# Two weight splits put behind the even tokens' normed x in a two-layer hybrid encoder

## The chip, the cores and the metric

The kernel runs on one core of one Trainium2 chip. The metric is the device time of one execution in microseconds (us), taken as the median of several runs. The profile is one further execution of the same program, recorded by the hardware profiler; its times count from the start of its span. PE is the matrix engine (TensorE), PEld its weight loads, DVE the vector engine, ACT the scalar engine, POOL the GpSimd engine and SP the engine whose queue issues most DMAs.

## The reference

A trunk of two layers on x of 1 x 256 x 1024 in float32. Each layer has two sub-layers, and each begins with an RMSNorm. The core of it:

```python
def _rmsnorm(x, g):
    xf = x.astype(jnp.float32)
    y = xf * lax.rsqrt(jnp.mean(xf * xf, axis=-1, keepdims=True) + EPS)
    return (y * g.astype(jnp.float32)).astype(x.dtype)

def _token_mixer(xn, w_in, w_pool, pool_scale, w_a, w_b, w_o, rel_bias):
    u, q, k, v, g_pool, g_attn = jnp.split(xn @ w_in, SPLITS, axis=-1)
    ...
    merged = jax.nn.sigmoid(g_pool) * (pool_out @ w_a) + jax.nn.sigmoid(g_attn) * (attn_out @ w_b)
    return merged @ w_o

def _conv_ffn(xn, w_up, conv_w, conv_b, w_down):
    a, gval = jnp.split(xn @ w_up, 2, axis=-1)
    ...
    return (jax.nn.gelu(a) * gval) @ w_down

def reference(x, ...):
    h = x
    for layer in range(DEPTH):
        h = h + _token_mixer(_rmsnorm(h, norm1[layer]), ...)
        h = h + _conv_ffn(_rmsnorm(h, norm2[layer]), ...)
    return _rmsnorm(h, norm_f)
```

The weights are some 170 MB in float32, and each is read once.

## The kernel before

**Products in parts.** A float32 operand is cut into a high part, rounded to the matrix engine's fast float32 form (fp32r), and a low part, the rest. A product is the sum of three: high by high, high by low and low by high. The activations stand as `x2`, 8 chunks of 128 channels, each with its two parts and with the 128 even and the 128 odd tokens apart (`t` = 0 and 1).

**Weights.** The class `Weights` brings them in a fixed order. `load` issues a DMA of 1 MB into one of three `raw` buffers (L137, on SP's queue), and each raw is split in two pieces: ACT copies the piece to `wh` (L201) and DVE subtracts that from the raw to get `wl` (L203, 128x1024). Five pairs of wh and wl buffers exist; some first pieces of a stage go into idle tiles instead, whose names are those of their tags (`m2`, `v1`, `ybig`, `at2`), so that the profile calls them m, v, ybig and at. `get` takes the next piece and splits up to three ahead. A raw buffer is free for the next load when both its pieces are split, so the load after next waits for the last DVE subtraction from it.

**Order within an engine.** Each engine runs its instructions in the order of its own program. That order is decided when the kernel is built, by a scheduler which takes the instructions by the times it reckons with. `tc.issue_after(inst)` adds a constraint to it: an instruction made in that block and on `inst`'s engine comes behind `inst` in that engine's program. It adds no wait on a semaphore. `queue_behind(insts, n)` notes such ties for the next `n` pieces that are split: every instruction in `insts` ties the part of the split that lies on its own engine. At most four such notes are kept.

**The residual product and the norm behind it.** `residual_mm` multiplies by `w_o` (8 chunks) or `w_down` (22 chunks) into four PSUM tiles, for two token parities and two halves of the 1024 columns. The last four chunks are held back and done parity by parity, in segments of columns: 512 and 512 for the even tokens, 512, 256 and 256 for the odd ones (PE L585 to L587). Behind each segment `Norm.add` runs: DVE adds the sum to h (L445), ACT squares it with a sum (L447, and its read-out as a second instruction), and POOL adds to the mean square (L454, L456). After the last segment of a parity POOL raises it to the power -1/2 (L459, tile `rstd`). For the third segment DVE first folds the sum of the early chunks into h (L631).

**The normed x.** The generator `fin` in `to_channels` follows. DVE multiplies h by rstd and the gain in four quarters of 256 columns (L472, `xn`), PE transposes four chunks of 128 columns into PSUM (L481, `xt_ps`), ACT copies them to the high part of x2 (L484) and DVE takes the low part (L485); then the same for the other four chunks. The generator stops once between the two halves, and `residual_mm` puts work between: for the even tokens, the odd tokens' last segment; for the odd tokens, the last step of `fill`. `fill` (`begin_mlp` or `begin_values`) starts the next stage for the even tokens: `v_sum` (L667) multiplies their x2 by four held pieces, 6 products a piece, in the order high x by wh, high x by wl, low x by wh. After the odd tokens come the same four pieces for them.

**Where it stands.** This norm with its transposes runs three times: in layer 0 behind w_o, at about 238 to 256 us of the span (called the first place below), in layer 0 behind w_down, at about 421 to 440 us (the second), and in layer 1 behind w_o, at about 663 to 680 us (the third). The final norm has a code of its own. Before the change `fin` ties the six pieces after it to the odd tokens' last copy and subtraction, and nothing to the even tokens'.

Of the kernel before, what the change touches and what calls it, by code (L numbers as in the profile page):

```python
# [241 lines left out]
def encoder(ctx, tc, x, w_in, w_pool, pool_scale, w_a, w_b, w_o, norm1, norm2, w_up, conv_w,  # L242
# [11 lines left out]
    W = Weights(tc, wpool, big)  # L254
# [208 lines left out]
    def to_channels(x2, psum, g):  # L463

        tag = "acc" if psum is acc else "mm"

        def fin(t, r, xn):
            for n in range(4):  # L470
                cc = slice(n * 256, (n + 1) * 256)
                nc.vector.scalar_tensor_tensor(  # L472
                    out=xn[:, cc], in0=h[:, t, cc], scalar=r[:, 0:1], in1=g[:, cc],
                    op0=ALU.mult, op1=ALU.mult,
                )
            for n in range(2):
                pt = psum.tile([P, 4, P], F32, tag=tag, name="xt_ps")
                ks = slice(4 * n, 4 * n + 4)
                for k in range(4):
                    c0 = (4 * n + k) * P  # L480
                    nc.tensor.transpose(pt[:, k, :], xn[:, c0 : c0 + P], ident)  # L481
                oh, ol = (x2[:, ks, part, t, :] for part in (0, 1))
                last = [
                    nc.scalar.copy(out=oh, in_=pt),  # L484
                    nc.vector.tensor_sub(out=ol, in0=pt, in1=oh.bitcast(F32)),  # L485
                ]
                if n == 0:
                    yield
            if t == 1:
                W.queue_behind(last, 6)  # L490

        return fin

# [870 lines left out]
```

## Time and profile before

| | |
|---|---|
| median of 3 runs | 862.62 us (862.19 to 862.68) |
| profiled execution | 862.26 us, with a span of 860.5 us |
| PE busy | 852.6 us (99%) |
| DVE busy | 618.8 us (72%) |
| ACT busy | 492.8 us (57%) |
| POOL busy | 32.7 us (4%) |
| HBM traffic | 216 GB/s over the span |
| granted PE clock | 0.999 of full speed |

Matmuls overlap in the records: one of 128x512 shows some 0.39 us, while the next begins 0.23 us after it. So a stretch of PE work is read from the starts of its instructions, and a "busy" PE can still wait. On DVE and ACT too an instruction may begin some 0.1 us before the recorded end of the one before.

### The profile page before, as it was taken

The numbers are of one execution on the slowest core, as the hardware profiler recorded it, in microseconds if no ns is written. First come the engines' busy times: TensorE is split into PE (matmuls) and PEld (weight loads), VectorE is DVE, ScalarE is ACT, GpSimd is POOL, SyncE is SP. The second block draws the span as 40 slices with busy tenths as digits, with TensorE's granted clock in tenths as the row PEclk, the third lists the DMA queues.
The fourth block names the chain that finished last, engine by engine and source line by source line (L and its number), as shares of the span: only waits on it lengthen the run. The fifth ranks groups of instructions, "written<-read, shape, count | busy, mean of one in ns | idle before, by whom it ended". The sixth has DMA issues, their size and how long they took to land.

```text
span 860.5 us, 11694 instructions
## 1 busy us (share of the span) xinstructions
PE 852.6 (99%) x4343; PEld 728.3 (85%) x4343; DVE 618.8 (72%) x946; ACT 492.8 (57%) x770; POOL 32.7 (4%) x98
## 2 busy tenths in 40 slices
PE   9999999999999999999999999999999999999997
PEld 8888888888888888888888889888888888888886
DVE  7998786557766787777755987764666766876774
ACT  7656665555445566566545666664554555755662
POOL 1800000000010000000000000000000100000001
PEclk9999999999999999999999999999999999999999
DMA  9686556776747786566626565657876387775741
GB/s 335 210 254 200 196 177 227 240 265 197 256 157 247 269 276 236 196 237 203 244 98 200 187 202 195 207 182 250 274 238 246 131 274 237 267 256 182 243 147 49
DMA packets 136384, 186.80 MB, mean 217 GB/s; under 512 B 5560, under 2 KB 88192, under 8 KB 136328
## 3 DMA queue, kind: packets, MB, share of 16 engines
q1 hardware_dynamic: 136168, 185.79, 64.4%
q8 instruction: 34, 0.56, 0.3%
q10 hardware_dynamic: 160, 0.27, 0.1%
q14 instruction: 22, 0.18, 0.1%
HBM read 172.39 MB, written 13.65 MB: 216 GB/s over the span
## 4 chain that ended last, share of the span: by engine, by line
PE 95%; DVE 2%; ACT 1%; issue 1%; DMA 1%; POOL 0%; POOLq 0%; ACTq 0%
PE proj_ps L543 33%; PE t_ps L667 30%; PE v_ps L667 6%; PE res_ps L587 5%; PE res_ps L585 5%; PE res_ps L586 5%; PE v_ps L895 3%; PE v_ps L802 1%; PE pool_ps L543 1%; PE o_ps L1083 1%; PE s_ps L1034 1%; PE s_ps L1029 1%; PE o_ps L1079 1%; DVE h L445 1%; DMA raw<-in_w_in_dram 1%
## 5 line engine op out<-in xcount | busy, mean ns | idle before, releaser
L203 DVE TENSOR_TENSOR wl<-raw,wh 128x1024 fp32r<-128x1024 f32 x274 | 331.9, 1220 | 134.8 <-ACT wh L201 109.0
L201 ACT CAST wh<-raw 128x1024 fp32r<-128x1024 f32 x274 | 284.9, 1050 | 132.4 <-PE t_ps L667 64.7
L543 PE MATMUL proj_ps<-x,wh 128*128 128x512 f32 x832 | 196.9, 390 | 0.0
L543 PEld LDWEIGHTS proj_ps<-x,wh 128*128 128x128 f32 x832 | 154.3, 188 | 30.9
L667 PE MATMUL t_ps<-wh,x 128*128 128x512 f32 x576 | 180.1, 390 | 0.0
L667 PEld LDWEIGHTS t_ps<-wh,x 128*128 128x128 f32 x576 | 108.2, 188 | 22.4
L667 PE MATMUL t_ps<-wl,x 128*128 128x512 f32 x288 | 112.0, 389 | 0.0
L543 PEld LDWEIGHTS proj_ps<-x,wl 128*128 128x128 f32 x832 | 105.4, 191 | 3.0
L543 PE MATMUL proj_ps<-x,wl 128*128 128x256 f32 x832 | 107.8, 283 | 0.0
L586 PE MATMUL res_ps<-wl,actq 128*128 128x512 f32 (+1 forms) x184 | 69.9, 380 | 0.0
L587 PE MATMUL res_ps<-wh,actk 128*128 128x512 f32 (+1 forms) x184 | 69.9, 380 | 0.0
L585 PE MATMUL res_ps<-wh,actq 128*128 128x512 f32 (+1 forms) x184 | 69.7, 381 | 0.0
L667 PEld LDWEIGHTS t_ps<-wl,x 128*128 128x128 f32 x288 | 54.1, 188 | 11.1
L667 PE MATMUL t_ps<-wh,po 128*128 128x512 f32 x128 | 41.4, 395 | 0.0
L587 PEld LDWEIGHTS res_ps<-wh,actk 128*128 128x128 f32 x184 | 34.6, 188 | 6.6
L586 PEld LDWEIGHTS res_ps<-wl,actq 128*128 128x128 f32 x184 | 34.6, 188 | 6.4
L585 PEld LDWEIGHTS res_ps<-wh,actq 128*128 128x128 f32 x184 | 34.5, 188 | 6.3
L579 ACT COPY a<-proj_ps 128x256 f32<-128x256 f32 x36 | 13.8, 388 | 37.4 <-PE proj_ps L543 37.4
L580 DVE TENSOR_TENSOR a<-proj_ps,a 128x256 f32<-128x256 f32 x36 | 15.0, 423 | 24.5 <-ACT a L579 24.4
L454 POOL TENSOR_SCALAR ss<-ss 128x1 f32<-128x1 f32 x8 | 1.9, 236 | 781.8 <-ACT junk L447 781.8
L667 PEld LDWEIGHTS t_ps<-wh,po 128*128 128x128 f32 x128 | 24.0, 188 | 4.9
L447 ACT ACTIVATE junk<-h 128x512 f32<-128x512 f32 (+1 forms) x19 | 10.5, 554 | 29.6 <-DVE h L445 29.5
(204 smaller groups left out, 1101.0 us busy)
## 6 DMA issues: line engine op xcount, KB each, us to landing
raw<-in_w_in_dram SPq DMA_DIRECT2D x58, 1024.0 KB, 5.8
raw<-in_w_up_dram SPq DMA_DIRECT2D x44, 1024.0 KB, 6.1
raw<-in_w_down_dram SPq DMA_DIRECT2D x22, 1024.0 KB, 4.9
raw<-in_w_a_dram SPq DMA_DIRECT2D x8, 1024.0 KB
raw<-in_w_o_dram SPq DMA_DIRECT2D x8, 1024.0 KB, 7.1
crossing<-crossing SPq DMA_DIRECT2D x12, 512.0 KB, 5.1
turning<-turning SPq DMA_DIRECT2D x8, 512.0 KB, 2.7
turned_p<-turning SPq DMA_DIRECT2D x32, 128.0 KB, 3.3
```

The costliest lines, as they stand in the source:

```text
L201: inst = nc.scalar.copy(out=h, in_=src)
L203: inst = nc.vector.tensor_sub(out=l, in0=src, in1=h.bitcast(F32))
L445: nc.vector.tensor_add(out=h[:, t, cc], in0=ps, in1=h[:, t, cc])
L447: nc.scalar.activation(junk[:, 0 : cc.stop - cc.start], h[:, t, cc], AF.Square, scale=D**-0.5, accum_out=ss[:, n : n + 1],)
L543: nc.tensor.matmul(out, w(k), x, start=(steps is first and k == 0), stop=(steps is last and k == nk - 1), skip_group_check=turns["rest"],)
L579: nc.scalar.copy(out=out, in_=sums[1])
L580: nc.vector.tensor_add(out=out, in0=sums[0], in1=out)
L585: nc.tensor.matmul(ps, ah, wh, start=first, stop=False, skip_group_check=on)
L586: nc.tensor.matmul(ps, ah, wl, start=False, stop=False, skip_group_check=on)
L587: nc.tensor.matmul(ps, al, wh, start=False, stop=last, skip_group_check=on)
L667: nc.tensor.matmul(ps, x2[:, 2 * n + j, part, t, :], w[:, j, :], start=(n + m == 0), stop=(n == last and m == 5),)
L895: nc.tensor.matmul(ps[t], a[:, k, t, :], w[:, j, :], start=(k + m == 0), stop=(k == KD - 1 and m == 2),)
```

## The change

`fin` now calls `queue_behind` after each parity, not after the odd tokens alone.

```diff
@@ -486,8 +486,7 @@
                 ]
                 if n == 0:
                     yield
-            if t == 1:
-                W.queue_behind(last, 6)
+            W.queue_behind(last if t else last[1:], 6 if t else 2)
 
         return fin
```

For the even tokens (`t` = 0) the next two pieces to be split are tied, and to `last[1:]` alone, the DVE subtraction of the low part of the second half (L485). So the DVE part of these two splits (L203) must come behind it in DVE's program; ACT's copies (L201) are not tied. For the odd tokens the tie is as before. In the built programs, PE, ACT, POOL and SP have the same instructions in the same order before and after. DVE's order differs at the three places, where one weight subtraction moves at each; the second of the two tied pieces already stood behind. In the first and the third place:

```
before                          after
L631 h (odd, second quarter)    L631 h
L203 wl                         L485 x (even, first half)
L485 x (even, first half)       L445 h (odd, last segment)
L445 h (odd, last segment)      L485 x (even, second half)
L485 x (even, second half)      L203 wl
L472 xn (odd) x4                L472 xn x4
```

In the second place:

```
before                          after
L445 h (even, first segment)    L445 h (even, first segment)
L203 wl                         L445 h (even, second segment)
L445 h (even, second segment)   L472 xn (even) x3
L472 xn (even)                  L445 h (odd, first segment)
L445 h (odd, first segment)     L472 xn (even)
L472 xn (even) x3               ...
...                             L485 x (even, second half)
L485 x (even, second half)      L203 wl
L472 xn (odd) x4                L472 xn (odd) x4
```

The waits on semaphores stay the same but for those that follow from the new order. On SP's queue, in the first and the third place, the load that takes the raw buffer from which this `wl` is made waits for it as before, and so for an instruction that stands later.

## The prediction
> **What bounds the kernel.** I read the page first: its span, its chain of waits, then the waits of PE.
>
> ```profile
> span 860.5 us, 11694 instructions
> PE 95%; DVE 2%; ACT 1%; issue 1%; DMA 1%; POOL 0%; POOLq 0%; ACTq 0%
> raw<-in_w_up_dram SPq DMA_DIRECT2D x44, 1024.0 KB, 6.1
> ```
> ```profile
> PE v_ps L667 <- DVE x L485: 0.8, 2, 0.4
> PE xt_ps L481 <- DVE xn L472: 0.5, 1, 0.5
> ```
>
> PE carries 95% of the chain, so only what PE waits for can be won. The second fence (engine, what it waited for, us, times, longest) has the two waits on DVE, at the three norms the change touches: twice a product waits for the low part of x, once a transpose for xn. A gap in the records is smaller than the loss, because a record outlasts the start of the next one. I therefore take losses from starts, in the timeline of PE at the first place:
>
> ```profile
> 245.10 0.60 PE L481 MATMUL xt_ps<-ident,xn 128*128 128x128 f32 x4
> 245.45 0.36 PE L585 MATMUL res_ps<-wh,m 128*128 128x256 f32 x1
> ...
> 247.33 0.71 PE L667 MATMUL v_ps<-v,x 128*128 128x512 f32 x2
> 248.43 1.20 PE L667 MATMUL v_ps<-v,x 128*128 128x512 f32 x4 [0.39 <-DVE x L485]
> 249.46 1.53 PE L667 MATMUL v_ps<-ybig,x 128*128 128x512 f32 x6
> ...
> 252.19 0.60 PE L481 MATMUL xt_ps<-ident,xn 128*128 128x128 f32 x4
> ...
> 252.86 0.40 PE L667 MATMUL v_ps<-wl,x 128*128 128x512 f32 x1
> ...
> 254.37 1.64 PE L667 MATMUL v_ps<-v,x 128*128 128x512 f32 x6
> 255.84 1.52 PE L667 MATMUL v_ps<-ybig,x 128*128 128x512 f32 x6
> ```
> ```profile
> 671.97 0.71 PE L667 MATMUL v_ps<-v,x 128*128 128x512 f32 x2
> ...
> 674.11 1.53 PE L667 MATMUL v_ps<-ybig,x 128*128 128x512 f32 x6
> ```
>
> The six products with piece v take 255.84 - 254.37 = 1.47 us for the odd tokens, where nothing is missing, and 249.46 - 247.33 = 2.13 us for the even ones. The loss is 0.66 us, and at the third place 674.11 - 671.97 - 1.47 = 0.67 us.
>
> **First and third place: the cause and the gain.** DVE, then ACT, then POOL around it:
>
> ```profile
> 246.55 1.22 DVE L203 TENSOR_TENSOR wl<-raw,wh 128x1024 fp32r<-128x1024 f32 x1
> 247.69 0.69 DVE L485 TENSOR_TENSOR x<-xt_ps,x 128x512 fp32r<-128x512 f32 x1
> 248.29 0.42 DVE L445 TENSOR_TENSOR h<-res_ps,h 128x256 f32<-128x256 f32 x1
> 248.62 0.68 DVE L485 TENSOR_TENSOR x<-xt_ps,x 128x512 fp32r<-128x512 f32 x1
> 250.33 1.67 DVE L472 SCALAR_TENSOR_TENSOR xn<-h,rstd,gain 128x256 f32<-128x256 f32 x4 [1.03 <-POOL rstd L459]
> ```
> ```profile
> 245.91 0.57 ACT L484 CAST x<-xt_ps 128x512 fp32r<-128x512 f32 x1
> ...
> 247.61 0.58 ACT L484 CAST x<-xt_ps 128x512 fp32r<-128x512 f32 x1 [0.69 <-PE xt_ps L481]
> 248.80 0.42 ACT L447 ACTIVATE junk<-h 128x256 f32<-128x256 f32 x1 [0.60 <-DVE h L445]
> 249.12 0.19 ACT L447 ACTIVATION_READ_ACCUMULATOR junk<-h 128x1 f32 x1
> ...
> 260.12 1.06 ACT L201 CAST wh<-raw 128x1024 fp32r<-128x1024 f32 x1 [1.09 <-PE v_ps L667]
> ```
> ```profile
> 247.06 0.76 POOL L456 TENSOR_TENSOR ss<-ss 128x1 f32<-128x1 f32 x1 [0.75 <-ACT junk L447]
> 249.45 0.20 POOL L456 TENSOR_TENSOR ss<-ss 128x1 f32<-128x1 f32 x1 [1.63 <-ACT junk L447]
> 249.72 0.57 POOL L459 TENSOR_TENSOR rstd<-ss,mhalf 128x1 f32<-128x1 f32 x1
> ```
>
> The high part was ready at 245.91 + 0.57 = 246.48, and DVE could have begun the low part at 246.55. The weight subtraction took that place, so the low part began at 247.69. With the weights gone from there it ends at 246.55 + 0.69 = 247.24. PE reaches its third product (the first that needs it) at about 247.33 + 2 x 0.25 = 247.8, 0.25 being 1.47/6. So the whole 0.66 us goes, and 0.67 us in the third place, where the order is the same.
>
> What is late next? The moved subtraction still costs its 1.22 us of DVE. The second low part waits for its copy, which ends at 247.61 + 0.58 = 248.19, whatever DVE does; it runs from 248.22 to 248.90, and the weights from 248.82 to 250.04. Three things stand behind them.
>
> First their own use, the product at 252.86 that comes to 252.20: 2.2 us in hand.
>
> Second the load that takes this raw buffer:
>
> ```profile
> 247.80 0.37 SPq L137 DMA_DIRECT2D raw<-in_w_up_dram  x1
> ```
>
> It was issued as the subtraction ended, and moves 2.27 us, to 250.07. Behind it on SP's queue stands the load of the next gain, which waits for the last xn anyway (250.33 + 1.67 = 252.00), so nothing is held up. The load lands, by the page's 6.1 us, at 256.2. Its first reader is the cast at 260.12 (the fifth after the odd tokens; PE released it), 259.5 after the gain. With 3.3 us in hand I cost it at 0. If that cover were gone, a late load would hold ACT's queue, one us for each us in the first and third places at most.
>
> Third the odd tokens' norm. The add to h moves from 248.29 to about 247.2. Its square follows the second copy on ACT, at 247.61 + 0.49 = 248.10 (the step by which ACT's next instruction follows such a copy; estimate) and not at 248.80, so all of POOL's steps come 0.70 us earlier: 248.75 and 249.02, and xn could start at 249.63. But DVE has the weights until 250.04, and POOL works under them. The row at 247.06 shows what that does: the same addition took 0.76 us under a weight subtraction and ended at 247.82, just past that one's end at 247.77; without it it took 0.20. So POOL gets through about 0.15 us before DVE's instruction ends. The power (0.57) would then run from 249.89 to 250.46, and xn begin at 250.50, 0.17 later than before. PE transposes at 252.19 - 0.66 = 251.53 and needs two quarters, ready at 250.50 + 0.88 (a step of 0.40 and a duration of 0.48) = 251.38: 0.15 in hand. If the addition is held as well, the power starts only after it, xn at 250.77, and the second quarter is ready at 251.65, against the third transpose at about 251.73. I take 0, the nearer row being an addition of 0.2 that starts before the weights do, and 0.2 us a place as the upper end.
>
> The Trainium skill (SBUF — State Buffer, "Who interferes with whom") says that a DVE instruction with two inputs in SBUF and a GpSimd one that reads SBUF exclude each other through a shared port, and that the one issued first holds it whole. The row at 247.06 agrees; by that rule POOL's addition, if first, would also hold up the weights by its 0.2 us, and the sum would stay within the upper end just given.
>
> **Second place.** Here another instruction is late:
>
> ```profile
> 424.47 1.23 DVE L203 TENSOR_TENSOR wl<-raw,wh 128x1024 fp32r<-128x1024 f32 x1 [1.94 <-ACT wh L201]
> 425.62 0.69 DVE L445 TENSOR_TENSOR h<-res_ps,h 128x512 f32<-128x512 f32 x1
> 428.14 0.48 DVE L472 SCALAR_TENSOR_TENSOR xn<-h,rstd,gain 128x256 f32<-128x256 f32 x1 [1.84 <-POOL rstd L459]
> ...
> 429.14 1.27 DVE L472 SCALAR_TENSOR_TENSOR xn<-h,rstd,gain 128x256 f32<-128x256 f32 x3
> ```
> ```profile
> 427.08 0.28 PE L585 MATMUL res_ps<-wh,actq 128*128 128x256 f32 x1
> ...
> 429.68 0.44 PE L481 MATMUL xt_ps<-ident,xn 128*128 128x128 f32 x2 [0.49 <-DVE xn L472]
> 429.87 0.37 PE L585 MATMUL res_ps<-wh,actq 128*128 128x256 f32 x1
> ...
> 435.94 0.60 PE L481 MATMUL xt_ps<-ident,xn 128*128 128x128 f32 x4
> ```
>
> In the first place the twelve narrow products take 245.10 - 243.66 = 1.44 us (the row of 243.66 stands below) and the four transposes 245.45 - 245.10 = 0.35. From 427.08 that makes 428.52 for the transposes and 428.87 for the next product, which came at 429.87. The loss is 1.00 us. Two causes add up. The h add ran straight behind the weights at 425.62. In the first place that add stands at
>
> ```profile
> 241.15 0.69 DVE L445 TENSOR_TENSOR h<-res_ps,h 128x512 f32<-128x512 f32 x1 [1.43 <-PE res_ps L587]
> ```
> ```profile
> 243.66 0.28 PE L585 MATMUL res_ps<-wh,m 128*128 128x256 f32 x1
> ```
>
> 2.51 us before the first narrow product, which here is 424.57. So it comes 1.05 us earlier, and xn, 2.52 behind it as before, at 427.09. The second quarter also stood behind an h add (429.14 after 428.14); it now follows at once, a step of 0.40 us later ((1.67 - 0.48)/3, from the row at 250.33), and is done at 427.97, half a us before PE needs it. So I take all of 1.00 us. The weights go behind the second low part, to about 432.3 to 433.5, and the odd tokens' power under them: by the steps of the first place the second quarter is ready at about 434.8, 0.3 before the third transpose (435.94 - 1.00 + 0.2). If the odd chain fails, 0.2 us at the upper end here too. These weights belong to the next group of columns, which PE takes up after the odd tokens' transposes, so they are no worry.
>
> **The sum.** 0.66 + 1.00 + 0.67 = 2.33 us off, 1.7 at the low end. PE's chain has no other wait behind these places, so the gain travels. The profiled execution was 862.26, its span and 1.76 around it; less 2.33 is 859.9. The median of the runs is 0.36 above it, which would make 860.3. I say 860.2.
>
> **Rivals.**
> *One place does not pay.* If the second place's transposes wait on (say POOL's chain and not DVE was late), only 1.33 us comes: about 861.1. For it, that place has two causes and needs both gone; against it, its chain goes step by step from the weights to xn.
> *PE's waits only change their name.* Each 0.66 is lost again at the odd tokens: 862.5. Against it, some margin at each step above; for it, that the margins at the transposes are 0.1 to 0.3 us.
> *POOL's chain becomes the bound: slower.* Say the addition and the power each pay the full stretch (0.76, and 0.57 + 0.56) and only after the weights: xn at 250.04 + 0.76 + 0.07 + 1.13 + 0.04 = 252.04, the second quarter and the step to PE 0.93 later, at 252.97, 1.24 after the third transpose wants it (251.73). That is 0.58 slower at the first and third place, and 1.24 - 1.00 = 0.24 at the second: +1.4, 863.9. It takes from the gain once xn begins after 250.80, and gives a loss from 251.46. By that port rule of the Trainium skill this goes too far, as one instruction ends the hold.
>
> **Chances.** The forecast 0.68, with 859.6 to 860.8 of its own; one place missing 0.14; nothing 0.10; slower 0.08. About 0.2% (1.7 us) can be told from no change: faster is below 860.9, slower above 864.3. The forecast gives 0.66 of faster and the missing place 0.04 (if it loses less); of the slower rival, which lies inside that bound, I still put most beyond it, since a price not seen would come there. The range of 859.5 to 861.6 leaves out the last two.
>
> **What would show it.** After: v products of the even tokens 1.47 us from the first to piece ybig, in both places; no wait of PE on x L485; the transposes of the second place without a break, xn there about 2.5 us after its h add; POOL's power under wl, stretched, and xn of the odd tokens near 250.5 on the old clock; the load 2.3 us later, with no wait for it on ACT. Wrong would be a PE wait at the odd tokens' transposes, or a wait for that load.

## The result, and the profile after

The changed kernel takes 859.98 us (median of 9 runs, 859.63 to 860.53) against 862.41 us of the kernel before (9 runs on the same chip): 2.43 us less, a ratio of 0.997 with a 95% interval of 0.996 to 0.998. The profiled execution took 859.98 us with a span of 858.2, 2.3 us shorter than before. The prediction was 860.2, in a range of 859.5 to 861.6.

From the page of the changed kernel, its span and its chain of waits, then the one wait that the view of PE's waits still lists (engine, what it waited for, us, times, longest). The file is one line shorter from L489 on, so that `v_sum` is L666 here.

```profile
span 858.2 us, 11696 instructions
PE 99%; ACT 0%; POOLq 0%; issue 0%; POOL 0%; ACTq 0%
```
```profile
PE gain_ps L372 <- PEq L1345: 0.8, 1, 0.8
```

PE's share of the chain went from 95% to 99%. That step, 4% of the span or some 34 us, is not the gain: followed back from a wait, the chain of before ran over DVE, ACT, POOL and a DMA (at the second place from 429.68 back to 406.42 us), while PE was busy beside them. Both waits on DVE are gone; what is left is the start of the program, which was there before. The timeline of PE at the first place (start, duration):

```profile
247.40 1.64 PE L666 MATMUL v_ps<-v,x 128*128 128x512 f32 x6
248.88 1.52 PE L666 MATMUL v_ps<-ybig,x 128*128 128x512 f32 x6
...
251.60 0.60 PE L481 MATMUL xt_ps<-ident,xn 128*128 128x128 f32 x4
251.96 0.48 PE L666 MATMUL v_ps<-wh,x 128*128 128x512 f32 x1
252.27 0.40 PE L666 MATMUL v_ps<-wl,x 128*128 128x512 f32 x1
```

The six v products of the even tokens stand in one row and take 1.48 us where they took 2.13, and the odd tokens' transposes follow at 251.60 with no wait. At the third place the same block takes 1.47 instead of 2.14:

```profile
670.37 1.64 PE L666 MATMUL v_ps<-v,x 128*128 128x512 f32 x6
671.84 1.52 PE L666 MATMUL v_ps<-ybig,x 128*128 128x512 f32 x6
```

DVE and POOL at the first place:

```profile
246.63 0.68 DVE L485 TENSOR_TENSOR x<-xt_ps,x 128x512 fp32r<-128x512 f32 x1
247.25 0.42 DVE L445 TENSOR_TENSOR h<-res_ps,h 128x256 f32<-128x256 f32 x1
248.31 0.69 DVE L485 TENSOR_TENSOR x<-xt_ps,x 128x512 fp32r<-128x512 f32 x1 [0.63 <-ACT x L484]
248.91 1.22 DVE L203 TENSOR_TENSOR wl<-raw,wh 128x1024 fp32r<-128x1024 f32 x1
250.59 1.67 DVE L472 SCALAR_TENSOR_TENSOR xn<-h,rstd,gain 128x256 f32<-128x256 f32 x4 [0.46 <-POOL rstd L459]
```
```profile
247.14 0.19 POOL L456 TENSOR_TENSOR ss<-ss 128x1 f32<-128x1 f32 x1 [0.75 <-ACT junk L447]
248.82 0.19 POOL L456 TENSOR_TENSOR ss<-ss 128x1 f32<-128x1 f32 x1 [1.49 <-ACT junk L447]
249.09 1.46 POOL L459 TENSOR_TENSOR rstd<-ss,mhalf 128x1 f32<-128x1 f32 x1
```

Two things are to be seen. The addition at 247.14, which took 0.76 us under the weights before, takes 0.19. In its place the power at 249.09 takes 1.46 instead of 0.57: it began 0.18 us after the weights did, and it ended at 250.55, 0.42 after they did (250.13). Both are of the odd tokens' norm: the hold moved there from the second addition to the power, the last step before xn, and PE shows no wait from it.

The second place, DVE and then PE:

```profile
423.97 0.69 DVE L445 TENSOR_TENSOR h<-res_ps,h 128x512 f32<-128x512 f32 x1 [2.03 <-PE res_ps L586]
426.50 1.28 DVE L472 SCALAR_TENSOR_TENSOR xn<-h,rstd,gain 128x256 f32<-128x256 f32 x3 [1.84 <-POOL rstd L459]
```
```profile
426.49 0.28 PE L584 MATMUL res_ps<-wh,actq 128*128 128x256 f32 x1
...
427.93 0.60 PE L481 MATMUL xt_ps<-ident,xn 128*128 128x128 f32 x4
428.28 0.36 PE L584 MATMUL res_ps<-wh,actq 128*128 128x256 f32 x1
```

The second add to h now waits for PE and not for the weights: it stands 426.49 - 423.97 = 2.52 us ahead of the first narrow product, xn comes 2.53 us behind it, and the transposes follow the twelve narrow products without a break. From the first narrow product to the one behind the transposes it is 428.28 - 426.49 = 1.79 us, and was 429.87 - 427.08 = 2.79.

The load that takes the raw buffer, on SP's queue, and ACT's first cast from it:

```profile
250.20 0.37 SPq L137 DMA_DIRECT2D raw<-in_w_up_dram  x1
```
```profile
259.54 1.06 ACT L201 CAST wh<-raw 128x1024 fp32r<-128x1024 f32 x1 [1.09 <-PE v_ps L666]
```

The load goes out 2.4 us later than before, and the cast is still released by PE and not by the DMA.

### The profile page after: what moved, and what is told of

It is laid out like the page before. It is cut to its first block, busy times and chain, and to the rows that moved or that the text cites. A ratio compares the mean times of both kernels' runs of the same rounds, so it can differ in the third digit from the quotient of the medians.

```text
span 858.2 us, 11696 instructions
## 1 busy us (share of the span) xinstructions
PE 851.7 (99%) x4343; PEld 728.6 (85%) x4343; DVE 619.2 (72%) x946; ACT 492.7 (57%) x770; POOL 33.1 (4%) x98
## 4 chain that ended last, share of the span: by engine, by line
PE 99%; ACT 0%; POOLq 0%; issue 0%; POOL 0%; ACTq 0%
PE proj_ps L542 34%; PE t_ps L666 30%; PE res_ps L586 6%; PE res_ps L584 6%; PE res_ps L585 6%; PE v_ps L666 6%; PE v_ps L894 3%; PE v_ps L801 1%; PE pool_ps L542 1%; PE o_ps L1082 1%; PE s_ps L1033 1%; PE s_ps L1028 1%; PE o_ps L1078 1%; PE xt_ps L481 1%; PE gain_ps L372 0%; PE xt_ps L749 0%
## 5 line engine op out<-in xcount | busy, mean ns | idle before, releaser
L203 DVE TENSOR_TENSOR wl<-raw,wh 128x1024 fp32r<-128x1024 f32 x274 | 331.9, 1220 | 132.0 <-ACT wh L201 106.1
L201 ACT CAST wh<-raw 128x1024 fp32r<-128x1024 f32 x274 | 284.9, 1050 | 132.3 <-PE t_ps L666 66.5
L666 PE MATMUL t_ps<-wh,x 128*128 128x512 f32 x576 | 180.1, 390 | 0.0
L666 PEld LDWEIGHTS t_ps<-wh,x 128*128 128x128 f32 x576 | 108.1, 188 | 22.5
L666 PE MATMUL t_ps<-wl,x 128*128 128x512 f32 x288 | 112.0, 389 | 0.0
L666 PEld LDWEIGHTS t_ps<-wl,x 128*128 128x128 f32 x288 | 54.1, 188 | 11.0
L666 PE MATMUL t_ps<-wh,po 128*128 128x512 f32 x128 | 41.4, 395 | 0.0
L666 PEld LDWEIGHTS t_ps<-wh,po 128*128 128x128 f32 x128 | 24.0, 188 | 4.9
L1272 ACT ACTIVATE y<-a,prm 128x256 f32<-128x256 f32 x44 | 25.1, 598 | 2.5 <-DVE a L579 2.2
```

The source lines that it names most:

```text
L201: inst = nc.scalar.copy(out=h, in_=src)
L203: inst = nc.vector.tensor_sub(out=l, in0=src, in1=h.bitcast(F32))
L666: nc.tensor.matmul(ps, x2[:, 2 * n + j, part, t, :], w[:, j, :], start=(n + m == 0), stop=(n == last and m == 5),)
L1272: nc.scalar.activation(y, a, AF.Identity, bias=b, scale=w1)
```

## Experiments

Theory: the gain is the sum of three local waits of PE, each of which ends because DVE no longer has the weights in front of what PE wants; the weights then hold POOL's power, within what the odd tokens' chain has in hand. Rivals: one place makes it all, or the odd tokens give part of it back, or the load matters. Each kernel is compared with the kernel before on the same chip. The first four ran together (35 runs of before, 862.41), then three (17 runs, 862.23), then one (15 runs, 862.25).

| kernel | runs | median us | less than before | ratio, 95% interval |
|---|---|---|---|---|
| tie at first and third place | 12 | 861.05 | 1.36 | 0.9984 (0.9975 to 0.9993) |
| tie at second place | 12 | 861.16 | 1.25 | 0.9987 (0.9977 to 0.9996) |
| weights twice | 12 | 861.77 | 0.64 | 0.9993 (0.9982 to 1.0004) |
| weights behind the odd tokens' xn | 12 | 860.75 | 1.66 | 0.9979 (0.9969 to 0.9989) |
| the changed kernel again | 6 | 859.73 | 2.50 | 0.9967 (0.9955 to 0.9978) |
| changed, old order of xn | 6 | 859.92 | 2.31 | 0.9971 (0.9959 to 0.9982) |
| weights behind the even tokens' add | 11 | 861.34 | 0.89 | 0.9987 (0.9978 to 0.9996) |
| before, new order of xn | 11 | 862.06 | 0.19 | 0.9997 (0.9988 to 1.0006) |

The intervals are some 0.8 to 1 us to each side, so that a step of a few tenths is read from PE's own timeline. For the second place one stretch serves for all kernels: from the first narrow product to the first product with piece ybig, which lies behind both of the even tokens' halves. It was 434.58 - 427.08 = 7.50 us before and 432.98 - 426.49 = 6.49 after.

### The places one by one

```diff
-            W.queue_behind(last if t else last[1:], 6 if t else 2)
+            if t or psum is acc:
+                W.queue_behind(last if t else last[1:], 6 if t else 2)
```

`psum is acc` holds at the first and the third place; the other kernel has `psum is mmp`, which holds at the second.

> The even tokens' tie is kept at the first and the third place and left out at the second. Theory (each place pays for itself): 0.66 + 0.67 = 1.33 us less than before, so about 861.1 where before is 862.4; PE's six v products of the even tokens step through in 1.47 us at both places, and at the second place the third transpose waits for xn as before, 1.0 us lost. Rival (the second place makes the whole gain, or PE loses at the odd tokens what it wins at the even ones): 862.4, with a wait of PE behind the first and third place.

> The tie is kept at the second place alone. Theory: 1.00 us less than before, about 861.4; the even tokens' transposes there begin without a break and the waits for x's low part stay at the first and third place. Rival (the second place does not pay, because POOL's chain and not DVE was late there): 862.4, and then the first and third place alone would have made 860.

With the first and third place alone, 1.36 us less was measured (1.33 expected). PE's timeline of that kernel, first place and then second:

```profile
247.39 1.64 PE L667 MATMUL v_ps<-v,x 128*128 128x512 f32 x6
248.86 1.52 PE L667 MATMUL v_ps<-ybig,x 128*128 128x512 f32 x6
```
```profile
426.47 0.28 PE L585 MATMUL res_ps<-wh,actq 128*128 128x256 f32 x1
...
429.04 0.44 PE L481 MATMUL xt_ps<-ident,xn 128*128 128x128 f32 x2 [0.49 <-DVE xn L472]
...
433.95 1.53 PE L667 MATMUL v_ps<-ybig,x 128*128 128x512 f32 x6
```

The v block takes 1.47 us, and the second place is as it was: a wait for xn, and 7.48 us for the stretch. With the second place alone it is the other way round: the v blocks take 2.15 and 2.13, the stretch 433.25 - 426.77 = 6.48. Its median is 1.25 us below before where 1.00 was expected, within its interval. The two parts sum to 2.61, the whole is 2.43 to 2.50: each place pays for itself, and none makes it all.

### The order of xn, or the add to h

The prediction named two causes at the second place: the late add to h, and the odd tokens' add standing between the first and the second quarter of xn. In the changed kernel both are gone. Two kernels put back, or take away, the second one alone.

```diff
+                late = psum is mmp and t == 0 and n >= 1
+                with tc.issue_after(W.added.ins) if late else ExitStack():
                     nc.vector.scalar_tensor_tensor(
                         out=xn[:, cc], in0=h[:, t, cc], scalar=r[:, 0:1], in1=g[:, cc],
```

`W.added` is the last add to h that was traced, here the odd tokens' first.

> As after the change, but at the second place the second to fourth quarter of the even tokens' xn stand behind the odd tokens' first add to h, which is the order of before. It tells the two causes named for that place apart. Theory now (the late add to h was the cause, the order of the quarters counts for nothing once that is gone): the second quarter ends at about 428.0 on the clock of after, and the third transpose wants it at 428.1, so the time is that of the changed kernel within 0.1 us, about 860.0. Rival (two causes that add up, as the prediction put it): 0.6 us of the second place's 1.0 comes back, 860.6.

859.92 us against 859.73 of the changed kernel beside it, and the stretch is 432.53 - 426.04 = 6.49, that of after to the hundredth. So the order of the quarters costs nothing once the add to h is early. The opposite kernel starts from the one before:

```diff
+                if n == NF and not whole and (t, m) == (1, 0):
+                    begun_xn, then = then(), None
+                    next(begun_xn)
...
+                with tc.issue_after(W.xn.ins) if begun_xn else ExitStack():
                     then = done(t, m, cc, res) or then
```

> The kernel before, with one difference: at the second place the odd tokens' first add to h stands behind three quarters of the even tokens' xn, the order of after, while the weight subtraction stays in front of the even tokens' second add to h. Theory (the two causes of the second place do not add up, they overlap: either one gone lets the second quarter come earlier, and with the add gone nothing is left for the order): the second quarter ends at about 429.0 on the clock of before and the third transpose follows at 429.1, not at 429.7, so 0.6 of the 1.0 us comes back: 0.6 less than before. Rival (the order of the quarters is worth nothing at all): the time of before, the third transpose at 429.7.

Both theories missed something. DVE of that kernel, then PE:

```profile
425.77 0.68 DVE L445 TENSOR_TENSOR h<-res_ps,h 128x512 f32<-128x512 f32 x1
428.29 1.28 DVE L472 SCALAR_TENSOR_TENSOR xn<-h,rstd,gain 128x256 f32<-128x256 f32 x3 [1.84 <-POOL rstd L459]
429.49 0.68 DVE L445 TENSOR_TENSOR h<-res_ps,h 128x512 f32<-128x512 f32 x1
...
431.51 0.69 DVE L487 TENSOR_TENSOR x<-xt_ps,x 128x512 fp32r<-128x512 f32 x1 [0.29 <-ACT x L486]
```
```profile
427.23 0.28 PE L587 MATMUL res_ps<-wh,actq 128*128 128x256 f32 x1
...
429.42 0.36 PE L587 MATMUL res_ps<-wh,actq 128*128 128x256 f32 x1
...
431.54 3.33 PE L676 MATMUL v_ps<-m,x 128*128 128x512 f32 x12
434.70 1.53 PE L676 MATMUL v_ps<-ybig,x 128*128 128x512 f32 x6
```

The transposes do come earlier: 429.42 - 427.23 = 2.19 us instead of 2.79, the 0.60 expected. But the odd tokens' add, now behind three quarters of xn, starts at 429.49; ACT squares behind it and only then copies the high part of x, at 430.92, and the low part follows at 431.51. The twelve products with m begin 0.26 us late (431.54, where 429.42 + 1.51 + 0.35 = 431.28 would do) and then take 3.16 us instead of 2.84. The stretch is 434.70 - 427.23 = 7.47, that of before. What the order gains at the transposes it loses at the products behind them, and the median (0.19 less, interval across 1) agrees.

### How little is enough at the second place

```diff
+                added = nc.vector.tensor_add(out=h[:, t, cc], in0=ps, in1=h[:, t, cc])
+                if self.tie and t == 0 and cc.stop == D:
+                    W.queue_behind((added,), 2)
...
-            W.queue_behind(last if t else last[1:], 6 if t else 2)
+            if t:
+                W.queue_behind(last, 6)
```

The lines are set against the changed kernel; `tie` is set for the norm of the second place alone.

> The tie of the change is left out everywhere. Instead, at the second place alone, the weight subtraction is tied behind the even tokens' second add to h, so that it runs while ACT and POOL make rstd. Theory: what counts at the second place is that add; it comes 1.05 us earlier, POOL's addition meets the end of the weights and loses at most 0.1, and the gain of 1.0 us is there without going behind x's low part: about 861.4. Rival (POOL is held through the weights and xn comes as late as before): 862.4.

DVE, then POOL, of that kernel:

```profile
425.80 0.69 DVE L445 TENSOR_TENSOR h<-res_ps,h 128x512 f32<-128x512 f32 x1 [2.03 <-PE res_ps L589]
426.41 1.22 DVE L203 TENSOR_TENSOR wl<-raw,wh 128x1024 fp32r<-128x1024 f32 x1
428.36 1.28 DVE L474 SCALAR_TENSOR_TENSOR xn<-h,rstd,gain 128x256 f32<-128x256 f32 x3 [0.73 <-POOL rstd L461]
```
```profile
427.45 0.22 POOL L458 TENSOR_TENSOR ss<-ss 128x1 f32<-128x1 f32 x1 [2.56 <-ACT junk L449]
427.75 0.57 POOL L461 TENSOR_TENSOR rstd<-ss,mhalf 128x1 f32<-128x1 f32 x1
```

The weights run while ACT squares, POOL's addition loses 0.03 us to them, and xn starts 2.56 us after the add instead of 2.53. The stretch is 434.80 - 428.32 = 6.48, and 0.89 us less was measured. Three quarters of xn stand ahead of the odd tokens' add here too; that counts for nothing once the even tokens' add is early, as shown above. So the whole gain of that place comes from one instruction that no longer stands ahead of the even tokens' second add.

### How much the odd tokens have in hand

```diff
                     inst = nc.vector.tensor_sub(out=l, in0=src, in1=h.bitcast(F32))
+                if n and i == self.twice:
+                    inst = nc.vector.tensor_sub(out=l, in0=src, in1=h.bitcast(F32))
```

The odd tokens' xn is tied behind the second subtraction, and PE's order is tied to that of the changed kernel.

> The moved weight subtraction runs twice in a row at each place, the odd tokens' xn comes behind the second, and PE's order is held as it is after the change. Theory (POOL's power waits under the weights and the odd tokens' chain has only 0.1 to 0.3 us in hand): xn begins 0.6 us later than after the change if POOL gets its turn between the two, 1.14 later if it waits for both, and PE's third transpose of the odd tokens comes 0.3 or 0.9 us late at each of the three places: 860.0 + 1.0 = 861.0, or 860.0 + 2.6 = 862.6. Rival (there is slack of a us or more at the odd tokens): 860.0, no wait of PE on xn. The load behind the weights goes out 1.2 us later without a wait for it.

DVE, POOL and PE of that kernel at the first place:

```profile
251.05 1.22 DVE L204 TENSOR_TENSOR wl<-raw,wh 128x1024 fp32r<-128x1024 f32 x1
252.30 1.23 DVE L206 TENSOR_TENSOR wl<-raw,wh 128x1024 fp32r<-128x1024 f32 x1
253.44 1.67 DVE L476 SCALAR_TENSOR_TENSOR xn<-h,rstd,gain 128x256 f32<-128x256 f32 x4
```
```profile
251.23 1.46 POOL L462 TENSOR_TENSOR rstd<-ss,mhalf 128x1 f32<-128x1 f32 x1
```
```profile
249.54 1.64 PE L673 MATMUL v_ps<-v,x 128*128 128x512 f32 x6
...
254.06 0.74 PE L485 MATMUL xt_ps<-ident,xn 128*128 128x128 f32 x4 [0.17 <-DVE xn L476]
254.56 0.49 PE L673 MATMUL v_ps<-wh,x 128*128 128x512 f32 x1
```

Counted from the v products, xn begins at 253.44 - 249.54 = 3.90 us, against 250.59 - 247.40 = 3.19 after the change: 0.71 later, where 0.6 was expected (the second subtraction writes the tile of the first and waits for it, so that it steps 1.25 us behind it and not 1.14). PE's product with wh comes 5.02 us after them instead of 4.56, so PE loses 0.46 us (0.3 expected), and 0.46 and 0.47 at the other two places. The chain therefore has 0.71 - 0.46 = 0.25 us in hand in the changed kernel. The power takes 1.46 us as with one subtraction: POOL got its turn at the end of the first. Three times 0.46 makes 1.39; the median is 1.79 above the changed kernel's 859.98, but this kernel's executions fall into two groups, 861.1 to 861.8 and 863.0 to 863.8, and the lower one is 1.1 to 1.8 above it. The profiled execution (863.84) is of the upper group and lost its 2 us in the first 12 us (below); that the others of the group lost theirs there too is not shown. The rival with a us in hand falls. What the load behind the weights did is told with the prediction's step on it (below).

```diff
+            if t == 1:
+                W.queue_behind((inst,), 2)
+                yield
             for n in range(2):
                 pt = psum.tile([P, 4, P], F32, tag=tag, name="xt_ps")
...
-        rest = fill() if fill else None
         half = then()
+        if fill:
+            next(half)
+        rest = fill() if fill else None
```

Here `inst` is the odd tokens' last quarter of xn, and the weights stand behind it. At the first and third place the load of the next gain now stands ahead of the raw buffer's load on SP's queue.

> The moved weight subtraction goes one step further, behind the odd tokens' four quarters of xn, at all three places. Theory (DVE's weights hold POOL's power): the power takes 0.57 us again, not 1.46, and xn begins 0.9 us earlier than after the change; PE gets nothing from it, since it was not waiting. At the first and third place the weights end at about 252.5 on the clock of after, and PE's first product with them wanted them at 252.27, so PE waits 0.3 us there: about 860.6 in all; at the second place no difference. Rival (the stretched power comes from something else): it stays at 1.46. Rival (the hold cost PE time after the change): faster than 859.98 at the second place by some tenths.

POOL, DVE and PE at the first place, whose v products begin at 246.96 in this kernel:

```profile
248.65 0.57 POOL L459 TENSOR_TENSOR rstd<-ss,mhalf 128x1 f32<-128x1 f32 x1
```
```profile
249.25 1.68 DVE L472 SCALAR_TENSOR_TENSOR xn<-h,rstd,gain 128x256 f32<-128x256 f32 x4 [0.70 <-POOL rstd L459]
250.84 1.22 DVE L203 TENSOR_TENSOR wl<-raw,wh 128x1024 fp32r<-128x1024 f32 x1
```
```profile
251.51 0.48 PE L671 MATMUL v_ps<-wh,x 128*128 128x512 f32 x1
252.11 0.50 PE L671 MATMUL v_ps<-wl,x 128*128 128x512 f32 x1
```

The power is back at 0.57, so it was DVE's weights that stretched it. xn begins 2.29 us after the v products, 0.90 earlier than after the change, and PE takes no notice: at the second place the step from the first product with m (430.12) to the odd tokens' (436.50) is 6.38 us, as in the changed kernel. At the first place the product with wl comes 0.60 us after the one with wh, where 0.31 was normal (251.96 to 252.27 above). 860.75 was measured, 0.77 above the changed kernel and 0.15 above what was expected. The expectation counted that first stall alone. From the even tokens' first v product to the odd tokens' it is 253.73 - 246.96 = 6.77 us here and 253.78 - 247.40 = 6.38 after the change, and at the third place 6.75 against 6.38: 0.76 us in all, against 0.77 by the medians. So at the first and third place the position that the change gives the weights has a wait of PE on either side: further forward, where the kernel before has them, for x's low part; further back for the weights themselves. Positions between that of before and that of the change were not tried. At the second place three positions (behind the even add, behind x's low part, behind the odd tokens' xn) cost PE nothing. No version here beats the changed kernel; PE has no wait left at these places.

## Why the prediction was right, and where a step of it was not

**The first and the third place.** The mechanism was right. The two losses of 0.66 and 0.67 us are gone (1.48 and 1.47 us for the block), and the kernel with these two alone gave 1.36 less. The reason is shown by taking the tie away at these places: the waits come back.

**The odd tokens' chain.** Its forecast came out step by step: xn at 250.50 on the old clock, and 250.59 here, with the whole place 0.07 later (247.40 against 247.33). The addition slipped in ahead of the weights, the power was held and stretched to 1.46 us. The prediction gave two figures for what is in hand there, 0.15 us against the first transpose and 0.30 in the slower rival (xn after 250.80); 0.25 was measured, so the upper end of 0.2 a place was not needed. That the addition, coming first, would hold up the weights by its 0.2 us did not happen (below).

**The load** went out 2.40 us later (0.07 of it the shift of the place), where 2.27 was reckoned, and cost nothing. With the weights twice it stood 1.3 us further back, and ACT's cast there was still released by PE. With the weights behind the odd tokens' xn it stood 2.4 us further back at the third place, issued at 675.51, and there the cast waited for it:

```profile
683.44 1.05 ACT L201 CAST wh<-raw 128x1024 fp32r<-128x1024 f32 x1 [1.69 <-DMA raw<-in_w_up_dram]
```

PE shows no wait from that either. The load took 683.44 - 675.51 = 7.93 us to the cast, with the gain's load ahead of it on the queue, where the prediction reckoned with 6.1. From the load to the cast it is 682.50 - 673.17 = 9.33 us at the third place of the changed kernel; by 7.93 it has 1.4 us in hand, where 3.3 were reckoned at the first place. The step that put the load at 0 held, on a smaller margin than was given.

**The second place.** The size was right: 7.50 - 6.49 = 1.01, with 1.00 forecast. The step "Two causes add up" was not. The late add to h is the only cause; the order of the quarters neither costs anything without it nor gains anything against it. The argument stopped at the second quarter of xn and did not follow the odd tokens' add, which the new order pushes back, into ACT's square and the high part that is copied behind it. In the changed kernel that path had room: the copy ended at 429.13 + 0.56 = 429.69, and PE's first product with m came at 430.14. The number survived because the first cause alone carries the whole 1.01; for the step that was wrong, that is luck.

**The sum.** 2.33 was forecast; 2.3 by the spans, 2.43 by the medians. The rival in which a place is missing fell with the first pair of kernels, and the one in which PE's waits only change their name with the result, as PE shows no wait on DVE any more. The slower one, POOL's chain as the bound, has its mechanism (the power is held) but not its price: it needs xn 0.25 us later before PE loses anything.

## What to carry to other kernels

When one engine carries nearly the whole chain, list its waits and look at what stands in front of the late instruction on the engine it waits for: a piece of work that nothing wants yet, moved back by a few places, can win the whole wait. Then follow the chain of everything that the move pushes back, on all engines up to the next use by the bounding one, since a gain at one instruction can be lost at the next. And measure what is in hand behind the new place by putting the same work there twice, and one place further on.

## What the runs showed of the hardware that was not expected

A DVE subtraction with both operands in SBUF holds back a POOL instruction that starts under it: the addition before (0.76 instead of 0.19), the power after (1.46 instead of 0.57). Such a power ends 0.42 us after the weights, less than its own 0.57, so by this estimate it begins its work about 0.15 before their recorded end. The other way round no hold is seen. In the changed kernel POOL's addition at 248.82 began ahead of the weights, and they still began at 248.91, 0.60 behind the low part at 248.31, and took their 1.22; with POOL idle the kernel before shows a step of 0.61 behind such a low part (255.27 to 255.88). With the weights twice, POOL's power ran on to 252.69 under the second subtraction, which took 1.23. That this one began 0.03 us after the end of the first, where DVE otherwise overlaps such pairs by some 0.1, is not POOL's doing: it waits for the first, and a DVE instruction that waits for the one before it shows the same 0.03 where POOL does nothing, as in the kernel before:

```profile
100.78 0.42 DVE L1131 SCALAR_TENSOR_TENSOR qkl<-proj_ps,kh 128x256 fp32r<-128x256 f32 x1 [1.38 <-ACT kh L1130]
101.23 0.42 DVE L1135 SCALAR_TENSOR_TENSOR qkl<-proj_ps,qkl 128x256 fp32r<-128x256 f32 x1
```

The Trainium skill (SBUF — State Buffer, "Who interferes with whom") lets the one that came first keep the port for its whole instruction. For the subtraction the trace agrees, but for its last 0.15 us; for POOL's addition and power it does not, as neither held DVE.

Executions also differ by 2 us and more before any of the places is reached. In the ten profiled ones the first product with piece at begins between 15.26 and 18.00 us, in the two of the changed kernel at 15.88 and 15.37. Here it is in that of the kernel with the weights twice, the latest, and then in one of the changed kernel:

```profile
18.00 0.39 PE L808 MATMUL v_ps<-at,xuh 128*128 128x512 f32 x1
```
```profile
15.88 0.39 PE L801 MATMUL v_ps<-at,xuh 128*128 128x512 f32 x1
```

Every engine has the same instructions in the same order up to there. In the first of the two PE's first transposes wait for x's load and the products behind them step more slowly; what sets this from one execution to the next was not tried. It is why a step of a few tenths is read here from a stretch of PE's timeline and not from a median.
